# The hidden tiles of a two-layer decoder trunk, placed 128 bytes further along each partition

## Chip, core and metric

The kernel runs on one core of one Trainium2 chip. The metric is device time in microseconds (us), the median of several executions. The engines are named as in the profile: PE (TensorE matmuls), PEld (TensorE weight loads), DVE (VectorE), ACT (ScalarE), POOL (GpSimd), SP (SyncE).

## What is computed

A decoder trunk of two layers over 256 tokens of width 1024, all in float32. Each layer is an attention followed by an MLP, each with a residual and a layer norm:

```python
def squared_relu_mlp(x, w_up, w_down):
    return jnp.square(jax.nn.relu(x @ w_up)) @ w_down
...
        h = layer_norm(DEEPNORM_ALPHA * h + mix, ln1_g[layer], ln1_b[layer])
        h = layer_norm(DEEPNORM_ALPHA * h + squared_relu_mlp(h, w_up[layer], w_down[layer]),
                       ln2_g[layer], ln2_b[layer])
```

`w_up` is 1024 x 4096 and `w_down` 4096 x 1024 in each layer. Layer 0 has a differential attention, layer 1 a block-sparse one, which at 256 tokens is one causal block.

## The kernel before

**Products.** Every float32 operand of a large product is split into a rounded part and a remainder (`act_hi` and `act_lo`, `whi` and `wlo`, `h_hi` and `h_lo`), and `three` issues three matmuls into one PSUM bank: high by high, high by low, low by high. With `moving_w` the activation is the stationary operand (it is loaded into the array, 128 x 128) and the weights stream past it, 512 columns a matmul; L141, L142 and L143 are these three. Without it the weights are stationary and the activation streams, 256 columns a matmul: L145, L146 and L147.

**Weights.** The weights of both layers come as 96 units of 128 x 2048 through a ring of `raw` tiles; ACT rounds each half unit (`whi`, L103) and DVE subtracts (`wlo`, L115). `bg` issues that work between matmuls.

**The MLP.** `mlp` works through the 4096 hidden columns in eight chunks `c` of 512. The first two chunks are computed with tokens on the partitions (`up_rows`), squared (`square`: tiles `relu`, `sqr`) and transposed on PE (`up_turn`, L776). From chunk 2 on, `up(c, j)` computes half a chunk with the weights stationary, 48 matmuls of 256 columns, and `up_out` squares and splits it into `h_hi` and `h_lo`. `down(c, j)` multiplies the hidden chunk by `w_down`: hidden tiles stationary, weights moving, 24 matmuls of 512 columns a call, 48 for both `j` (half as many where it takes one half of the tokens). From chunk 3 on the order is written out by hand: `down(c - 3, 0)`, `down(c - 3, 1)`, `up(c, 0)`, `up(c, 1)`. In layer 1 the last quarter of the output is done in two pieces of 256 columns in the banks `ps_b` (`rest`).

**Places in SBUF.** The pools are stacked: constants (`act_hi`, `act_lo`, `xres`, `ident`), then the weights' pool (`raw`, `whi`, `wlo`, `bias`), then small tiles, then on top either the attention's pool or the MLP's, in the same bytes. Within a pool the tiles stand in the order in which their names are first asked for. In the MLP's pool that is `relu` (2 buffers of 2 KB a partition), `sqr` (2 of 2 KB), `h_hi` (3 of 4 KB), `h_lo` (3 of 4 KB). Counted in bytes from the start of a partition, every `whi`, `wlo` and `raw` tile begins 192 bytes past a multiple of 512; `act_hi`, `act_lo`, `xres`, `ident`, `relu`, `sqr`, `h_hi` and `h_lo` begin 128 bytes past one. In the attention's pool `t` begins 128 past a multiple and `o` 192 past. Each slice that a matmul takes starts a whole number of 512 bytes into its tile, so the slices stand as their tiles do.

Of the kernel before, what the change touches and what calls it, by code (L numbers as in the profile page):

```python
# [20 lines left out]
F32 = mybir.dt.float32  # L21
# [7 lines left out]
P = 128  # L29
# [23 lines left out]
def trunk(ctx: ExitStack, tc: tile.TileContext, x, first, units, lam_a, subln, rel_bias,  # L53
# [686 lines left out]
    def mlp(layer, u0, then):  # L740
# [3 lines left out]
        with tc.tile_pool(name=f"mlp{layer}", bufs=2) as pool:  # L744
            H, acc, rest, SQ = {}, {}, {}, {}

            def hidden(c):
                H[c] = (pool.tile([P, 4, S], F32R, name="h_hi", bufs=3),
                        pool.tile([P, 4, S], F32R, name="h_lo", bufs=3))
# [20 lines left out]
            def up_turn(c, h):  # L770
                if h == 0:
                    hidden(c)
                src = SQ.pop((c, h))
                pt = bank("c")
                for j in range(4):
                    nc.tensor.transpose(pt[:, j * P:(j + 1) * P], src[:, j * P:(j + 1) * P], ident)  # L776
                split_to(H[c][0][:, :, tokens(h)], H[c][1][:, :, tokens(h)],
                         pt.rearrange("p (j t) -> p j t", j=4))

            def up(c, j):  # L780
                if j == 0:
                    hidden(c)
                u = u0 + [0, 2, 4, 8, 12, 16, 20, 24][c] + j
                hi, lo = unit(u, k=NK)
                ps = bank("b")
                for m in range(2):
                    w = slice(m * P, (m + 1) * P)
                    for k in range(NK):
                        three(ps[:, m * S:(m + 1) * S], (hi[:, k, w], lo[:, k, w]),
                              (act[0][:, k], act[1][:, k]), False, 1 / 16, k == 0, k == NK - 1)  # L790
                used.add(u)
                SQ[c, j] = ps
# [110 lines left out]
    with tc.manual_schedule(engines=engines):  # L903
        attention(0, 0)
        mlp(0, 16, lambda: ln_params(1))
        attention(1, UNITS)
        mlp(1, UNITS + 16, None)
# [73 lines left out]
```

## Time and profile before

| | |
|---|---|
| median of 3 runs | 593.27 us (593.0 to 593.7) |
| the profiled execution, its own time | 593.63 us |
| its span, first to last instruction | 591.6 us |
| outside the span | 2.0 us |
| mean granted TensorE clock | 0.995 of full speed |
| PE busy | 580.2 us, 98% of the span |
| PEld busy | 515.6 us, 87% |
| DVE, ACT busy | 378.5 us, 318.3 us |
| DMA | 113.03 MB, 191 GB/s on average |

Matmuls overlap in the profile: the duration of one counts its way through the array, and the next starts before it ends. The pace of a stream of matmuls is therefore read from the starts of two of them and the number between, not from the durations.

### The profile page before, as it was taken

To read this page: it belongs to the slowest core of one execution; us is meant where nothing else is said; L and a number is where in the kernel's file an instruction comes from. 1 tells how busy PE (TensorE), PEld (TensorE's weight loads), DVE (VectorE), ACT (ScalarE), POOL (GpSimd) and SP (SyncE) were. 2 spreads that over 40 slices of the span, in tenths; PEclk is the share of its full clock that TensorE was granted. 3 is DMA by queue.
4 is the path that set the end of the run, shared out by engine and by line. 5 is a ranking of instruction groups with operands and counts; after the bars stand their busy time and mean duration, and the time that the engine had idled before them with its cause. 6 is when DMAs were issued, how large, how long until landed. Compare 5 with 4: busy or idle time off the path is not lost.

```text
span 591.6 us, 9649 instructions
## 1 busy us (share of the span) xinstructions
PE 580.2 (98%) x3768; PEld 515.6 (87%) x3768; DVE 378.5 (64%) x692; ACT 318.3 (54%) x540; POOL 13.1 (2%) x45
## 2 busy tenths in 40 slices
PE   9999999999999999999999999999999999999993
PEld 7999978889899899898889999878899899899883
DVE  5798778976744644543978677697785544554236
ACT  6676787257654655552447555642785564554100
POOL 2000020000000000000000000000000000000000
PEclk9999999999999999999999999999999999999998
DMA  8996736447745836755259744151798556553002
GB/s 300 327 337 229 243 116 212 174 150 268 271 172 207 277 126 237 248 168 191 83 170 344 256 150 155 54 178 36 242 324 288 175 183 214 187 170 107 1 0 71
DMA packets 35548, 113.03 MB, mean 191 GB/s; under 512 B 3872, under 2 KB 8880, under 8 KB 35504
## 3 DMA queue, kind: packets, MB, share of 16 engines
q1 hardware_dynamic: 34144, 107.95, 53.8%
q0 software_dynamic: 1152, 4.19, 2.4%
q8 instruction: 29, 0.48, 0.3%
q10 hardware_dynamic: 208, 0.29, 0.1%
q14 instruction: 15, 0.12, 0.1%
HBM read 111.35 MB, written 1.07 MB: 190 GB/s over the span
## 4 chain that ended last, share of the span: by engine, by line
PE 97%; DMA 1%; DVE 1%; ACT 0%; SPq 0%; issue 0%; DVEq 0%
PE ps_a L143 13%; PE ps_a L142 13%; PE ps_b L145 13%; PE ps_a L141 13%; PE ps_b L147 12%; PE ps_b L146 12%; PE ps_b L141 4%; PE ps_b L143 4%; PE ps_b L142 4%; PE ps_a L462 2%; PE ps_c L515 1%; PE ps_c L292 1%; DMA raw<-in_first 1%; PE ps_a L550 1%; PE ps_c L776 1%; PE ps_a L381 1%
## 5 line engine op out<-in xcount | busy, mean ns | idle before, releaser
L115 DVE TENSOR_TENSOR wlo<-raw,whi 128x1024 fp32r<-128x1024 f32 x188 | 222.8, 1220 | 55.1 <-ACT whi L103 54.7
L103 ACT ACTIVATE whi<-raw 128x1024 fp32r<-128x1024 f32 x188 | 190.1, 1052 | 71.6 <-PE ps_a L143 52.5
L145 PE MATMUL ps_b<-act_hi,whi 128*128 128x256 f32 x640 | 179.8, 281 | 0.0
L146 PE MATMUL ps_b<-act_lo,whi 128*128 128x256 f32 x640 | 177.5, 277 | 0.0
L147 PE MATMUL ps_b<-act_hi,wlo 128*128 128x256 f32 x640 | 177.5, 277 | 0.0
L145 PEld LDWEIGHTS ps_b<-act_hi,whi 128*128 128x128 f32 x640 | 120.2, 188 | 1.5 <-issue 0.7
L146 PEld LDWEIGHTS ps_b<-act_lo,whi 128*128 128x128 f32 x640 | 120.7, 189 | 0.5
L147 PEld LDWEIGHTS ps_b<-act_hi,wlo 128*128 128x128 f32 x640 | 120.3, 188 | 0.0
L143 PE MATMUL ps_a<-whi,h_lo 128*128 128x512 f32 x248 | 97.7, 394 | 0.0
L142 PE MATMUL ps_a<-wlo,h_hi 128*128 128x512 f32 x248 | 97.2, 392 | 0.0
L141 PE MATMUL ps_a<-whi,h_hi 128*128 128x512 f32 x248 | 96.5, 389 | 0.0
L74 DVE TENSOR_TENSOR h_lo<-sqr,h_hi 128x512 fp32r<-128x512 f32 x24 | 16.6, 693 | 77.7 <-ACT h_hi L72 77.7
L142 PEld LDWEIGHTS ps_a<-wlo,h_hi 128*128 128x128 f32 x248 | 46.6, 188 | 10.3
L141 PEld LDWEIGHTS ps_a<-whi,h_hi 128*128 128x128 f32 x248 | 46.6, 188 | 9.9
L143 PEld LDWEIGHTS ps_a<-whi,h_lo 128*128 128x128 f32 x248 | 46.6, 188 | 9.3
L753 ACT ACTIVATE relu<-ps_b 128x512 f32<-128x512 f32 x32 | 19.1, 596 | 65.9 <-PE ps_b L147 55.0
L482 ACT ACTIVATE t<-t,mx 128x256 f32<-128x256 f32 x64 | 28.4, 445 | 31.5 <-DVE mx L479 31.5
L141 PE MATMUL ps_b<-whi,act_hi 128*128 128x512 f32 x96 | 39.1, 407 | 0.0
L143 PE MATMUL ps_b<-whi,act_lo 128*128 128x512 f32 x96 | 37.7, 393 | 0.0
L142 PE MATMUL ps_b<-wlo,act_hi 128*128 128x512 f32 x96 | 37.6, 391 | 0.0
L141 PE MATMUL ps_a<-whi,act_hi 128*128 128x512 f32 x80 | 32.3, 403 | 0.0
L142 PE MATMUL ps_a<-wlo,act_hi 128*128 128x512 f32 x80 | 31.5, 393 | 0.0
(140 smaller groups left out, 587.3 us busy)
## 6 DMA issues: line engine op xcount, KB each, us to landing
raw<-in_units SPq DMA_DIRECT2D x188, 512.0 KB, 4.6
bias<-scr SPq DMA_DIRECT2D x16, 256.0 KB, 5.3
lnp<-in_ln_g POOLq DMA_DIRECT2D x4, 512.0 KB, 4.5
lnp<-in_ln_b POOLq DMA_DIRECT2D x4, 512.0 KB, 5.4
raw<-in_first SPq DMA_DIRECT2D x5, 384.0 KB, 6.6
xres<-in_x SPq DMA_DIRECT2D x1, 1024.0 KB, 5.9
out<-xres SPq DMA_DIRECT2D x2, 256.0 KB, 2.1
out<-xres SPq DMA_DIRECT2D x4, 128.0 KB, 1.9
```

Source lines behind the costliest of these rows:

```text
L74: nc.vector.tensor_tensor(lo, src, hi.bitcast(F32), op=ALU.subtract)
L103: nc.scalar.activation(split[v][0][:, c], raws[state["head"]], AF.Copy)
L115: nc.vector.tensor_tensor(split[v][1][:, c], raws.pop(state["piece"]), split[v][0][:, c].bitcast(F32), op=ALU.subtract)
L141: nc.tensor.matmul(ps, a[0], w[0], start=start, stop=False)
L142: nc.tensor.matmul(ps, a[0], w[1], start=False, stop=False)
L143: nc.tensor.matmul(ps, a[1], w[0], start=False, stop=stop)
L145: nc.tensor.matmul(ps, w[0], a[0], start=start, stop=False)
L146: nc.tensor.matmul(ps, w[0], a[1], start=False, stop=False)
L147: nc.tensor.matmul(ps, w[1], a[0], start=False, stop=stop)
L462: nc.tensor.matmul(sc[m][:, c:c + n], a[r, q], b[r, :n], start=i == 0, stop=i == 2)
L482: nc.scalar.activation(t[:, m, s], t[:, m, s], AF.Exp, bias=mx[:, m, j:j + 1], accum_out=sm[:, m, j:j + 1])
L753: nc.scalar.activation(r, ps, AF.Relu)
```

## The change

One tile of 32 float32 a partition (128 bytes) is asked for first in the MLP's pool of each layer. Nothing reads or writes it. `relu`, `sqr`, `h_hi` and `h_lo` then begin 128 bytes later, at 256 past a multiple of 512; every tile of the lower pools stays where it was.

```diff
@@ -744,6 +744,8 @@
         with tc.tile_pool(name=f"mlp{layer}", bufs=2) as pool:
             H, acc, rest, SQ = {}, {}, {}, {}
 
+            pool.tile([P, 32], F32, name="pad", bufs=1)
+
             def hidden(c):
                 H[c] = (pool.tile([P, 4, S], F32R, name="h_hi", bufs=3),
                         pool.tile([P, 4, S], F32R, name="h_lo", bufs=3))
```

## Rows read from the trace of the kernel before

**Rows 1.** The page: busy time of the engines, and the chain that ended last by line.

```profile
PE 580.2 (98%) x3768; PEld 515.6 (87%) x3768; DVE 378.5 (64%) x692; ACT 318.3 (54%) x540; POOL 13.1 (2%) x45
...
PE ps_a L143 13%; PE ps_a L142 13%; PE ps_b L145 13%; PE ps_a L141 13%; PE ps_b L147 12%; PE ps_b L146 12%; PE ps_b L141 4%; PE ps_b L143 4%; PE ps_b L142 4%; PE ps_a L462 2%; PE ps_c L515 1%; PE ps_c L292 1%; DMA raw<-in_first 1%; PE ps_a L550 1%; PE ps_c L776 1%; PE ps_a L381 1%
```

**Rows 2.** Waits of PE, first and last of four: us in total, times, longest.

```profile
PE ps_c L186 <- DVE lnp L179: 1.2, 1, 1.2
...
PE ps_a L381 <- ACT whi L72: 0.2, 1, 0.2
```

**Rows 3.** Groups by line and shape, whole run: busy us, mean ns | idle before.

```profile
L143 PE MATMUL ps_a<-whi,h_lo 128*128 128x512 f32 x248 | 97.7, 394 | 0.0
L142 PE MATMUL ps_a<-wlo,h_hi 128*128 128x512 f32 x248 | 97.2, 392 | 0.0
L141 PE MATMUL ps_a<-whi,h_hi 128*128 128x512 f32 x248 | 96.5, 389 | 0.0
...
L776 PEld LDWEIGHTS ps_c<-ident,sqr 128*128 128x128 f32 x32 | 3.9, 140 | 0.8
...
L74 DVE TENSOR_TENSOR wlo<-raw,whi 128x512 fp32r<-128x512 f32 x5 | 3.5, 693 | 0.1
...
L292 PEld LDWEIGHTS ps_c<-ident,o 128*128 128x128 f32 x16 | 1.8, 140 | 1.8 <-ACT aT L524 0.8 <-ACT V L349 0.7
```

**Rows 4.** Timeline of PE, one pair of `down` calls: start us, duration us.

```profile
172.38 0.39 PE L142 MATMUL ps_a<-wlo,h_hi 128*128 128x512 f32 x1
...
182.68 0.39 PE L142 MATMUL ps_a<-wlo,h_hi 128*128 128x512 f32 x1
```

**Rows 5.** Timeline of PE, one pair of `up` calls that follows a `down`.

```profile
161.25 0.28 PE L145 MATMUL ps_b<-act_hi,whi 128*128 128x256 f32 x1
...
161.84 0.28 PE L147 MATMUL ps_b<-act_hi,wlo 128*128 128x256 f32 x1
...
172.04 0.28 PE L147 MATMUL ps_b<-act_hi,wlo 128*128 128x256 f32 x1
```

**Rows 6.** Timeline of PE, the pair of `up` calls for chunk 2.

```profile
138.73 0.28 PE L147 MATMUL ps_b<-act_hi,wlo 128*128 128x256 f32 x1
...
149.69 0.28 PE L147 MATMUL ps_b<-act_hi,wlo 128*128 128x256 f32 x1
```

**Rows 7.** Timeline of PE, end of layer 0's attention.

```profile
98.94 0.60 PE L292 MATMUL ps_c<-ident,o 128*128 128x128 f32 x4
...
99.85 0.40 PE L143 MATMUL ps_b<-whi,act_lo 128*128 128x512 f32 x1
...
111.05 0.40 PE L143 MATMUL ps_a<-whi,act_lo 128*128 128x512 f32 x1
```

**Rows 8.** Timeline of PE, the two 256-column pieces at the end of layer 1.

```profile
576.99 0.28 PE L141 MATMUL ps_b<-whi,h_hi 128*128 128x256 f32 x1
...
582.09 0.28 PE L141 MATMUL ps_b<-whi,h_hi 128*128 128x256 f32 x1
```

**Rows 9.** By tile (`h_hi`, `h_lo`, `relu`, `sqr`): ns min/median/max, first and last start.

```profile
L753 ACT ACTIVATE relu<-ps_b x32: 577/598/599, 120.0 to 549.7; 128x512 f32<-128x512 f32 x32
L755 ACT ACTIVATE sqr<-relu x32: 630/632/634, 120.6 to 550.3; 128x512 f32<-128x512 f32 x32
L72 ACT ACTIVATE h_hi<-sqr x24: 631/632/635, 145.6 to 551.0; 128x512 fp32r<-128x512 f32 x24
L74 DVE TENSOR_TENSOR h_lo<-sqr,h_hi x24: 691/693/694, 146.3 to 551.7; 128x512 fp32r<-128x512 f32 x24
L143 PEld LDWEIGHTS ps_a<-whi,h_lo x248: 187/188/188, 150.5 to 576.5; 128*128 128x128 f32 x124
```

**Rows 10.** Windows: length, busy us (instructions) of PE, PEld, DVE, ACT, POOL; granted clock, DMA, GB/s.

```profile
100.00:150.00 50.00, 50.00 (x281) 43.07 (x280) 40.10 (x63) 28.40 (x37) 1.17 (x2) 1.00 0.62 210
150.00:200.00 50.00, 50.00 (x319) 44.98 (x318) 27.88 (x27) 30.67 (x38) 0.00 (x0) 1.00 0.61 215
```

**Rows 11.** Timeline of DVE around the first `down`.

```profile
140.04 0.69 DVE L74 TENSOR_TENSOR h_lo<-ps_c,h_hi 128x512 fp32r<-128x512 f32 x1 [2.99 <-ACT h_hi L72]
```

## The prediction, made before the changed kernel was run

> **What bounds the kernel now.** I read the page first, for the busy shares and the chain that ended last, then the waits of PE, then the timeline of PE stretch by stretch. PE is busy for 98% of the span, and the chain is a list of matmul lines [rows 1]: the kernel lasts as long as PE needs to issue its 3768 matmuls. PE itself waits four times, the longest wait 1.2 us, and every one of the four is at the start of the program or around layer 0's attention; none has a tile of the MLP in it [rows 2]. So a change that only moves tiles can act in two ways: it changes the spacing of the matmuls that read those tiles, or it makes a producer of them so late that PE begins to wait.
>
> The spacing is what the reader should look at. In a pair of `down` calls the L142 matmuls that start at 172.38 and 182.68 are 45 matmuls apart (15 groups of three): 10.30 / 45 = 228.9 ns for 512 columns [rows 4]. In a pair of `up` calls the two L147 at 161.84 and 172.04 are 90 apart: 10.20 / 90 = 113.3 ns for 256 columns [rows 5]. But the same two kinds of stream also run at a second, slower beat. The `up` calls of chunk 2 take 10.96 us for 93 matmuls, 117.8 ns each [rows 6], and 48 matmuls of layer 0's output projection take 11.20 us, 233.3 ns each [rows 7]. So a matmul is about 4.4 ns (512 columns) or 4.5 ns (256 columns) dearer on the slow beat. The granted clock is 1.00 around both beats [rows 10], so the clock is not what separates them. Neither is the place of the operands: `up` of chunk 2 [rows 6] and `up` of chunk 3 [rows 5] read the same `act` tiles and weights' tiles that stand alike. A stream falls into a beat when it starts and keeps it: the first six starts of the `up` at 161.25 span 0.59 us, 118 ns each, and the rest of that stretch runs at 113.3 [rows 5].
>
> **The change part by part.**
>
> *Instructions.* The new tile is neither written nor read. No instruction, DMA or queue entry is added or moved: 0 us.
>
> *Matmuls with hidden tiles as the stationary operand.* These are 3 x 248 = 744 of 512 columns [rows 3] and 48 of 256 columns. Before, stationary tile and moving weights stand at 128 and 192 past a multiple of 512 bytes: the weights are 64 bytes ahead. After, it is 256 and 192: they are 64 bytes behind. The trace holds both arrangements, though not for 512 columns. In `up` the moving `act` stands at 128 and the stationary weights at 192, so the moving side is 64 bytes behind, as it will be in `down` after the change: 113.3 ns [rows 5]. In the last 48 matmuls of layer 1 the hidden tile is stationary and the weights move, 64 bytes ahead: the L141 at 576.99 and 582.09 are 45 apart, 5.10 / 45 = 113.3 ns [rows 8]. The two are the same to the resolution of the rows, and they differ in the relative place by just the 128 bytes of this change. I take 0 from this. The bounds: as a loss, that all 744 fall to the slow beat, 744 x 4.4 = 3.3 us. As a gain, that a 512-column matmul comes down to twice the 256-column one, 226.6 ns: 744 x 2.3 = 1.7 us.
>
> A page would allow a larger effect. The row gives 228.9 ns for 512 columns [rows 4]. The Trainium skill, "TensorE: Matmul & The Clock Gate", section "Wait — 56ns, not 53.3ns?", gives N / 2.4 + about 2.5 ns from start to start of matmuls back to back, measured there as 215.7 ns at 512 columns. By the page 13.2 ns of each gap would be a surplus, and if it came from where the two operands stand and the shift removed it, the sum would be an estimated 744 x 13.2 = 9.8 us less, 583.5 us. The row does not say where that surplus comes from.
>
> *Weight loads.* They take 187 to 188 ns with hidden tiles [rows 9], and loads are hidden under the running matmul. The transposes of `sqr` load in 140 ns from 128 past a multiple, and those of `o` in the same 140 ns from 192 past [rows 3]: 0 us for the 32 of them.
>
> *ACT and DVE.* Per half chunk `relu` 598, `sqr` 632, `h_hi` 632 and `h_lo` 693 ns [rows 9]; the subtraction of a weight of the same shape, whose tiles stand 64 bytes elsewhere, takes the same 693 ns [rows 3]. I take 0. The cover is large in any case. For chunk 0 the last `h_lo` is written from 140.04 us, done at 140.7 [rows 11], and the first `down` loads its `h_lo` at 150.5 [rows 9]: over 9 us of cover against 0.7 us of work. For chunk 7 the last `h_lo` is done at 551.7 + 0.7 = 552.4, and its `up` ended at about 549.7, when `relu` began [rows 9]; 48 matmuls of `down(5)` and 24 of one token half of chunk 6 come first, 72 x 228.9 ns = 16.5 us, so it is first read at about 566, 13 us after it is done. A producer would have to become nine us later before PE waits; without any cover a half chunk would cost the 2.6 us of these four instructions in a row.
>
> *Old neighbours.* The MLP's tiles lie where attention's tiles lay. Shifted by 128 bytes, the third `h_hi` reaches into the old `o`, the first `h_lo` into the old `V`. The transposes of `o` before the MLP are at 98.94 [rows 7], and `h_hi` from chunk 2 is first written at 145.6 [rows 9]: over 40 us lie between. 0 us.
>
> The sum is 0, against the 593.63 us of the profiled execution (span 591.6 and 2.0 outside). That execution lies 0.36 us above the median of 593.27. I predict the median, 593.3.
>
> **The rivals.**
>
> *Slower: the hidden tiles push the matmuls to the slow beat.* The place is the boundary where `down` starts after `up`, the price 4.4 ns a matmul, and it decides as soon as one more stall per matmul appears between the load and the moving stream. For it: both beats occur in this trace with 512 columns [rows 4, 7], and 512 columns with the new relative place are not in the trace. Against it: rows 5 and 8 as above. If the `down` calls alone are hit: 593.3 + 3.3 = 596.6. A `down` on the slow beat may also hand it to the five `up` pairs that follow one in each layer, 10 x about 90 matmuls x 4.5 = 4.1 us more: 600.7.
>
> *Faster: the shift ends part of the 228.9.* For it: 512 columns cost 2.3 ns more than twice 256. Against: that surplus may belong to the length of the stream, and nothing in the trace ties it to the tiles' place. With 1.7 us gained: 591.6. The page named above would allow 583.5; I give that 0.02 of the gain's chance, since the rows show no 512-column stream faster than 228.9 ns.
>
> *The beats after a transpose flip.* Chunk 2's `up` follows the transposes of `sqr`, and it is slow in both layers (I show layer 0's). The moved `sqr` could start it on the fast beat: 2 x 93 x 4.5 = 0.8 us, 592.4, which stays within the bound of no change.
>
> *The change does nothing at all,* if the tile were placed behind the others: 593.3, the same forecast by another way.
>
> **How the numbers follow.** What a measurement here can tell from no change is about 0.2%, 1.2 us. The forecast of no effect, with the flip after the transposes and the tile that moves nothing, has 0.68: 592.1 to 594.5. The slow beat has 0.19, of which `down` alone 0.12 and `down` with `up` 0.07. A gain over 1.2 us has 0.13. So faster 0.13, same 0.68, slower 0.19. The range goes from 592.0 to 596.8: it takes in the forecast and the slow beat in the `down` calls, 0.80, and leaves out the gain and the slow beat everywhere.
>
> **What would show it.** Right: in the profile after, a pair of `down` calls still has 228.9 ns between starts, the mean of the L141 to L143 groups stays at 389 to 394 ns, `up` after a `down` stays at 113.3, and PE waits no more than before. Wrong on the slow side: `down` at about 233, the means of these groups near 398. Wrong on the fast side: `down` below 228. The prediction is wrong above all if a 512-column stream reacts to a place that a 256-column stream does not notice.

## The result, and the profile after

The changed kernel takes 598.59 us (median of 5 runs, 597.66 to 599.16) against 593.70 us (median of 5, 593.00 to 593.86): 1.0082 times the time before, interval 1.0071 to 1.0094. It is slower by 0.8%. The forecast of no effect, 593.3 us, was wrong, and the time lies above the range, which ended at 596.8. The rival "the hidden tiles push the matmuls to the slow beat" is what happened, as far as the times go; its two prices, 596.6 and 600.7, lie on either side of the measured time.

The profiled execution has its own time of 599.16 us and a span of 597.1, 5.5 us longer than before. The page shows the same picture: PE is busy for 98% of the span and the chain is PE's matmul lines.

```profile
PE 584.9 (98%) x3768; PEld 517.0 (87%) x3768; DVE 378.1 (63%) x692; ACT 318.9 (53%) x540; POOL 12.9 (2%) x45
...
PE ps_a L141 13%; PE ps_a L143 13%; PE ps_a L142 13%; PE ps_b L145 13%; PE ps_b L147 12%; PE ps_b L146 12%; PE ps_b L141 4%; PE ps_b L143 4%; PE ps_b L142 4%; PE ps_a L462 2%; PE ps_c L515 1%; PE ps_c L292 1%; DMA raw<-in_first 1%; PE ps_a L550 1%; PE ps_c L778 1%; PE ps_a L381 1%
```

The waits of PE are the same four (us in total, times, longest). None belongs to the MLP. The one that grew, by 0.8 us against [rows 2], is the first weight tile at the start of the program, ahead of anything that the change touches; the first 256-column stream starts 0.5 us later for it (at 17.07 us, before at 16.56).

```profile
PE ps_c L186 <- DVE lnp L179: 1.2, 1, 1.2
PE ps_a L381 <- ACT whi L72: 1.0, 1, 1.0
PE ps_c L292 <- ACT aT L524: 0.6, 1, 0.6
PE ps_c L292 <- ACT V L349: 0.4, 1, 0.4
```

Beyond that half microsecond PE does not wait longer: the matmuls themselves are further apart. By line and shape, the three groups of `down` (means 389, 392 and 394 ns in [rows 3]) are now:

```profile
L141 PE MATMUL ps_a<-whi,h_hi 128*128 128x512 f32 x248 | 98.2, 396 | 0.0
L143 PE MATMUL ps_a<-whi,h_lo 128*128 128x512 f32 x248 | 98.1, 395 | 0.0
L142 PE MATMUL ps_a<-wlo,h_hi 128*128 128x512 f32 x248 | 98.0, 395 | 0.0
```

The timeline of PE gives the spacing. Below stand, in this order, the `up` pair of chunk 3 (two L145 that are 87 matmuls apart), a `down` pair (two L141, 39 apart), the `up` pair of chunk 4 (87 apart), layer 1's first attention projection (87 apart) and the 256-column pieces at the end (39 apart).

```profile
162.66 0.28 PE L145 MATMUL ps_b<-act_hi,whi 128*128 128x256 f32 x1
...
172.52 0.28 PE L145 MATMUL ps_b<-act_hi,whi 128*128 128x256 f32 x1
...
174.25 0.40 PE L141 MATMUL ps_a<-whi,h_hi 128*128 128x512 f32 x1
...
183.36 0.39 PE L141 MATMUL ps_a<-whi,h_hi 128*128 128x512 f32 x1
184.76 0.28 PE L145 MATMUL ps_b<-act_hi,whi 128*128 128x256 f32 x1
...
195.01 0.28 PE L145 MATMUL ps_b<-act_hi,whi 128*128 128x256 f32 x1
...
320.29 0.28 PE L145 MATMUL ps_b<-act_hi,whi 128*128 128x256 f32 x1
...
330.15 0.28 PE L145 MATMUL ps_b<-act_hi,whi 128*128 128x256 f32 x1
...
582.96 0.28 PE L141 MATMUL ps_b<-whi,h_hi 128*128 128x256 f32 x1
...
587.55 0.28 PE L141 MATMUL ps_b<-whi,h_hi 128*128 128x256 f32 x1
```

`down`: 9.11 / 39 = 233.6 ns, where [rows 4] has 228.9; over all stretches it is 233.2 to 233.4, and no `down` of either layer is at 229. It is slow straight after an `up` on the fast beat (chunk 3: 9.86 / 87 = 113.3). Of the ten `up` pairs that follow a `down`, six are still at 113.3 and four have gone to the slow beat, those of chunks 4 and 6 in each layer (10.25 / 87 = 117.8). The last 48 matmuls go from 113.3 [rows 8] to 4.59 / 39 = 117.7. Two stretches that read no hidden tile slow down as well: the 39 matmuls of `act` right after layer 0's last `down` go from 228.6 to 233.4, and layer 1's second projection (48 matmuls) from 113.2 to 117.6. One stretch went the other way: layer 1's first projection runs at 9.86 / 87 = 113.3, and ran at 10.25 / 87 = 117.8 before:

```profile
317.16 0.28 PE L145 MATMUL ps_b<-act_hi,whi 128*128 128x256 f32 x1
...
327.41 0.28 PE L145 MATMUL ps_b<-act_hi,whi 128*128 128x256 f32 x1
```

The sum, each stretch counted from its first start to the first start of what follows it: `down` 3.2 us, the four `up` pairs 4 x 0.41 = 1.6, the last 48 matmuls 0.2, the 39 of `act` 0.2, layer 1's two projections 0.2 - 0.4, the start of the program 0.5: 5.5 us, against 5.5 of span. Without the start it is 5.0, and the medians differ by 4.9. The granted clock is 0.996 over the span, as before (0.995).

### The profile page after: what moved, and what is told of

Read it like the earlier page. It is cut to its first block, busy times and chain, and to the rows that moved or that the text cites. A ratio compares the mean times of both kernels' runs of the same rounds, so it can differ in the third digit from the quotient of the medians.

```text
span 597.1 us, 9649 instructions
## 1 busy us (share of the span) xinstructions
PE 584.9 (98%) x3768; PEld 517.0 (87%) x3768; DVE 378.1 (63%) x692; ACT 318.9 (53%) x540; POOL 12.9 (2%) x45
## 4 chain that ended last, share of the span: by engine, by line
PE 97%; DMA 1%; DVE 1%; ACT 0%; SPq 0%; issue 0%; DVEq 0%
PE ps_a L141 13%; PE ps_a L143 13%; PE ps_a L142 13%; PE ps_b L145 13%; PE ps_b L147 12%; PE ps_b L146 12%; PE ps_b L141 4%; PE ps_b L143 4%; PE ps_b L142 4%; PE ps_a L462 2%; PE ps_c L515 1%; PE ps_c L292 1%; DMA raw<-in_first 1%; PE ps_a L550 1%; PE ps_c L778 1%; PE ps_a L381 1%
## 5 line engine op out<-in xcount | busy, mean ns | idle before, releaser
L145 PE MATMUL ps_b<-act_hi,whi 128*128 128x256 f32 x640 | 180.2, 282 | 0.0
L145 PEld LDWEIGHTS ps_b<-act_hi,whi 128*128 128x128 f32 x640 | 120.4, 188 | 1.5 <-issue 0.7
L141 PE MATMUL ps_a<-whi,h_hi 128*128 128x512 f32 x248 | 98.2, 396 | 0.0
L141 PEld LDWEIGHTS ps_a<-whi,h_hi 128*128 128x128 f32 x248 | 46.6, 188 | 10.7
L141 PE MATMUL ps_b<-whi,act_hi 128*128 128x512 f32 x96 | 39.2, 408 | 0.0
L141 PE MATMUL ps_a<-whi,act_hi 128*128 128x512 f32 x80 | 32.4, 405 | 0.0
L143 PE MATMUL ps_a<-whi,act_lo 128*128 128x512 f32 x80 | 31.5, 394 | 0.0
```

Source lines behind the costliest of these rows:

```text
L141: nc.tensor.matmul(ps, a[0], w[0], start=start, stop=False)
L143: nc.tensor.matmul(ps, a[1], w[0], start=False, stop=stop)
L145: nc.tensor.matmul(ps, w[0], a[0], start=start, stop=False)
```

## Experiments

**Which of the moved tiles it is, and seen from where.** Four kernels, each an edit of the kernel before.

A pad of 512 bytes instead of 128: the tiles move four times as far and stand at 128 past a multiple of 512 again.

```diff
+            pool.tile([P, 128], F32, name="pad", bufs=1)
```

> The pad in the MLP's pool is 512 bytes instead of 128, so its tiles move four times as far but stand at 128 past a multiple of 512 again. Place theory (where a hidden tile begins within 512 bytes, seen from the weights, sets the spacing of the 512-column matmuls): back to before, 593.7 us, down at 228.9 ns a matmul. Rival, any shift upsets the beats (another order of overlaps with attention's old tiles, another way into the stream): about 598 us or some third value, down not at 228.9 throughout.

Measured: 593.91 us, ratio 1.0006 (0.9997 to 1.0015). Two L141 of a `down` pair, 39 apart, are 8.93 us apart, 229.0 ns:

```profile
173.78 0.39 PE L141 MATMUL ps_a<-whi,h_hi 128*128 128x512 f32 x1
...
182.71 0.39 PE L141 MATMUL ps_a<-whi,h_hi 128*128 128x512 f32 x1
```

A move as such is harmless; new overlaps with attention's old tiles are not the cause.

Only `h_hi` and `h_lo` moved by 128 bytes, then only `relu` and `sqr`:

```diff
 # hidden tiles only
             def hidden(c):
+                if c == 0:
+                    pool.tile([P, 32], F32, name="padh", bufs=1)
 # relu and sqr only: 128 bytes ahead of them, 384 more ahead of h_hi
+            pool.tile([P, 32], F32, name="pad", bufs=1)
...
             def hidden(c):
+                if c == 0:
+                    pool.tile([P, 96], F32, name="padh", bufs=1)
```

> Only h_hi and h_lo stand 128 bytes further; relu and sqr keep their places. Place theory: the whole loss stays, 598 to 599 us, down at 233.3 ns. Rival, the transposes of the moved sqr start the streams on the slow beat, which is then handed on: 593.7 us, down at 228.9.

> relu and sqr stand 128 bytes further, h_hi and h_lo 512 bytes further, which is the same place within 512. Place theory: 593.7 us within 1 us, down at 228.9; up of chunk 2 may change its beat by up to 0.8 us for both layers. Rival of the transposes of sqr: 598 to 599 us.

Measured: hidden tiles only, 598.63 us, 1.0088 (1.0074 to 1.0102), `down` at 9.10 / 39 = 233.3 ns, the same four `up` pairs slow. `relu` and `sqr` only: 593.49 us, 1.0000 (0.9991 to 1.0009), `down` at 8.92 / 39 = 228.7. The transposes of `sqr` and ACT's work on `relu` and `sqr` have no part in it. The rows are of the first of the two:

```profile
173.96 0.40 PE L141 MATMUL ps_a<-whi,h_hi 128*128 128x512 f32 x1
...
183.06 0.39 PE L141 MATMUL ps_a<-whi,h_hi 128*128 128x512 f32 x1
```

Everything from `act_hi` upwards moved by 128 bytes, the weights too:

```diff
+    const.tile([P, 32], F32, name="padc")
     act = (const.tile([P, NK, S], F32R, name="act_hi"), const.tile([P, NK, S], F32R, name="act_lo"))
```

> Everything from act_hi upwards, weights included, stands 128 bytes further, so the hidden tiles are at 256 past a multiple of 512 as in the change and the weights at 320: the relative places are those of before. Relative place decides: 593.7 us, down at 228.9. Rival, the hidden tile's own place (256 past a multiple) decides: down at 233.3, 597 us or more.

Measured: 593.72 us, 1.0006 (0.9997 to 1.0015). The hidden tiles stand at 256 past a multiple of 512, as in the change, and `down` is at 8.93 / 39 = 229.0:

```profile
194.57 0.39 PE L141 MATMUL ps_a<-whi,h_hi 128*128 128x512 f32 x1
...
203.50 0.39 PE L141 MATMUL ps_a<-whi,h_hi 128*128 128x512 f32 x1
```

So it is not the hidden tiles' own place but their place seen from tiles that were moved with them here. Of these `act` drops out by the kernels further down: there the weights and the hidden tiles move together, away from `act`, and `down` stays at 228.9. What is left is the weights' pool, which holds `whi` and `wlo`, that PE reads, and `raw` and `bias`, that it does not.

Could writes of the other engines or of DMA do it, by meeting PE's reads? The profile of the changed kernel has 10 us of `down` in which DVE, ACT and POOL are idle and the DMA share is 0.01. The spacing there is 9.10 / 39 = 233.3 all the same, so the writes are not needed for it, and the tiles that count are `whi` and `wlo`:

```profile
560.00:570.00 10.00, 10.00 (x45) 8.05 (x44) 0.00 (x0) 0.00 (x0) 0.00 (x0) 1.00 0.01 2
...
560.55 0.39 PE L141 MATMUL ps_a<-whi,h_hi 128*128 128x512 f32 x1
...
569.65 0.40 PE L141 MATMUL ps_a<-whi,h_hi 128*128 128x512 f32 x1
```

**The other places.** Pads of 64, 256, 384 and 192 bytes (`[P, 16]`, `[P, 64]`, `[P, 96]`, `[P, 48]` in the same line).

> Pad of 64 bytes: the hidden tiles begin at 192 past a multiple of 512, exactly where the weights begin. If the loss comes from hidden tiles standing behind the weights, this is the border case: down at 228.9 ns and 593.5 us if the border belongs to the good side, 233.3 and 598 us if to the bad. If two reads that start at the same place collide most, it is the worst of all: over 233.3 ns, over 599 us.

> Pad of 256 bytes: hidden tiles at 384, weights at 192, so 192 bytes behind. If the pattern repeats every 256 bytes this is the place of before (64 ahead): 593.5 us, down at 228.9. If it repeats only every 512 and being behind is what costs: 598 us, down at 233.3.

> Pad of 384 bytes: hidden tiles at 0, weights at 192, so 192 bytes ahead. If the pattern repeats every 256 bytes this is the place of the change (64 behind): 598 us, down at 233.3. If it repeats every 512 and being ahead is good: 593.5 us, down at 228.9.

> Pad of 192 bytes: the stationary hidden tiles begin 128 bytes behind the weights, the one place of the four within 256 bytes not yet seen (64 ahead gave 228.9 ns in down, level 226.7, 64 behind 233.3). If the spacing rises steadily from level to behind: at or over 233.3 ns, 598 us or more. If the two sides of half the period are alike: between 228.9 and 233.3, 594 to 598 us. The last 48 matmuls of 256 columns go with it (113.3 ns at 64 ahead, 117.8 at 64 behind, 119.8 level).

Measured, with the change and the kernel before in their places; "ahead" and "behind" say where the weights' tiles begin, seen from the hidden tiles, within 256 bytes. "Level" means that both begin at the same byte within 256. The spacings are means of a steady stretch in ns, good to about 0.3; the ratio's interval stands in brackets.

| pad, bytes | weights | `down` | ten `up` pairs after a `down` | last 48 | us | ratio |
|---|---|---|---|---|---|---|
| 0 (before) | 64 ahead | 228.9 | 113.3 all | 113.3 | | 1 |
| 64 | level | 226.7 | 117.8 all | 120.0 | 595.23 | 1.0028 (1.0018 to 1.0038) |
| 128 (the change) | 64 behind | 233.3 | 117.8 in four | 117.8 | 598.59 | 1.0082 (1.0071 to 1.0094) |
| 192 | 128 away | 232.1 to 232.5 | 117.8 all | 118.7 | 600.07 | 1.0103 (1.0088 to 1.0118) |
| 256 | 64 ahead again | 228.9 | 113.3 all | 113.3 | 593.56 | 1.0000 (0.9991 to 1.0009) |
| 384 | 64 behind again | 233.3 | 117.8 in four | 117.8 | 598.90 | 1.0090 (1.0075 to 1.0105) |

The two places that were tried twice, 256 bytes apart, agree, down to which `up` pairs are slow; for the other two the period of 256 bytes is taken over, not shown. The level place is the best for `down`, and the whole gain of it and more is lost in the `up` pairs behind it. Timeline of the pad of 64 bytes: a `down` pair (39 apart, 8.84 / 39 = 226.7), the `up` pair after it (87 apart, 10.24 / 87 = 117.7), the last 48 (39 apart, 4.68 / 39 = 120.0):

```profile
173.42 0.39 PE L141 MATMUL ps_a<-whi,h_hi 128*128 128x512 f32 x1
...
182.26 0.39 PE L141 MATMUL ps_a<-whi,h_hi 128*128 128x512 f32 x1
183.65 0.28 PE L145 MATMUL ps_b<-act_hi,whi 128*128 128x256 f32 x1
...
193.89 0.28 PE L145 MATMUL ps_b<-act_hi,whi 128*128 128x256 f32 x1
...
579.08 0.28 PE L141 MATMUL ps_b<-whi,h_hi 128*128 128x256 f32 x1
...
583.76 0.28 PE L141 MATMUL ps_b<-whi,h_hi 128*128 128x256 f32 x1
```

The same pair of `down` rows with the pad of 256 bytes (8.93 / 39 = 229.0):

```profile
173.59 0.39 PE L141 MATMUL ps_a<-whi,h_hi 128*128 128x512 f32 x1
...
182.52 0.39 PE L141 MATMUL ps_a<-whi,h_hi 128*128 128x512 f32 x1
```

and with the pad of 192 bytes (9.07 / 39 = 232.6):

```profile
174.49 0.40 PE L141 MATMUL ps_a<-whi,h_hi 128*128 128x512 f32 x1
...
183.56 0.39 PE L141 MATMUL ps_a<-whi,h_hi 128*128 128x512 f32 x1
```

**Does each load pay for itself?** Only `h_lo` moved, by 128 bytes; then `h_hi` and `h_lo` set apart, one of them level with the weights.

```diff
 # only h_lo by 128 bytes; with [P, 16] h_lo is level and h_hi as before
+                hi = pool.tile([P, 4, S], F32R, name="h_hi", bufs=3)
+                if c == 0:
+                    pool.tile([P, 32], F32, name="padl", bufs=1)
+                H[c] = (hi, pool.tile([P, 4, S], F32R, name="h_lo", bufs=3))
 # h_hi level: [P, 16] as the pool's first tile and [P, 48] ahead of h_lo
```

> Only h_lo stands 128 bytes further. One load in three of down then has the place of the change. If each load pays for its own place, a third of the loss of down: 248 x 4.4 ns = 1.1 us, 594.6 us, down near 230.4 on average. If the beat belongs to the stream as a whole, all or nothing: 593.5 or 597 to 599 us.

> h_hi 64 bytes ahead of the weights as before, h_lo level with them. If each load pays for its own place: down (2 x 228.9 + 226.7) / 3 = 228.2 ns, 0.5 us less, 593.2 us, with up as before at 113.3. If the stream follows one of the two as a whole: 228.9 or 226.7, and up at 117.8 behind a down of 226.7, 593.7 or 595.2 us.

> h_hi level with the weights, h_lo 64 bytes ahead. Each load for itself: (2 x 226.7 + 228.9) / 3 = 227.4 ns, 1.1 us less, 592.6 us if up stays at 113.3, 596 us if it goes to 117.8. As a whole: 228.9 or 226.7.

Measured. Only `h_lo` by 128: 596.35 us, 1.0047 (1.0030 to 1.0064); `down` at 9.09 / 39 = 233.1, all ten `up` pairs at 9.86 / 87 = 113.3. One misplaced load in three costs `down` as much as three, and the difference to the change lies for the most part in the `up` pairs (1.7 us).

```profile
183.76 0.28 PE L145 MATMUL ps_b<-act_hi,whi 128*128 128x256 f32 x1
...
193.62 0.28 PE L145 MATMUL ps_b<-act_hi,whi 128*128 128x256 f32 x1
...
195.37 0.40 PE L141 MATMUL ps_a<-whi,h_hi 128*128 128x512 f32 x1
...
204.46 0.40 PE L141 MATMUL ps_a<-whi,h_hi 128*128 128x512 f32 x1
```

`h_lo` level: 597.78 us, 1.0074 (1.0062 to 1.0087), `down` at 8.95 / 39 = 229.5 (two L141 at 173.17 and 182.12), all ten `up` pairs at 117.8. `h_hi` level: 594.41 us, 1.0012 (1.0003 to 1.0021), `down` at 9.00 / 39 = 230.8 (two L141 at 194.98 and 203.98), all ten at 113.3. Both expectations are missed: neither do the loads add up one by one, nor does the stream take one tile's value.

**Does the rule hold for other operands?** The weights and all above them moved away from `act_hi` and `act_lo`, by 64 and by 128 bytes; the hidden tiles keep their place relative to the weights. Seen from `act`, the weights then begin 128 away, and 64 behind within 256.

```diff
     nlam = const.tile([P, 1], F32, name="nlam")
+    const.tile([P, 16], F32, name="padw")   # 64 bytes; [P, 32]: 128 bytes
```

> 64 bytes between the constants and the weights: weights, hidden tiles and attention's tiles move together, only act, xres and ident stay. Down keeps its relative place: 228.9 ns. The act tiles stand 128 bytes from the weights instead of 64. If the rule of relative place holds for any operand: the output and value products of attention (512 columns, act stationary) take the spacing that a pad of 192 bytes shows for down, and up (256 columns, act moving) a new one for all its matmuls. Rival, only the hidden tiles react: 593.6 us, up and attention as before.

> 128 bytes between the constants and the weights: hidden tiles stay 64 ahead of the weights, act tiles stand 192 ahead, which is 64 behind within 256. Rule of relative place: down 228.9 ns; attention's 576 matmuls of 512 columns with act stationary at 233.3 (2.3 us more); up with its weights 64 ahead of the moving act now always at 113.3 ns, no slow stretch (1.7 us less). Together 594 us. Rival, only hidden tiles react: 593.6 us with the slow up stretches where they were.

Measured. By 64: 604.94 us, 1.0183 (1.0168 to 1.0198). Nine of the ten `up` pairs are at 10.44 / 87 = 120.0 (two L145 at 187.22 and 197.66), the tenth at 118.7. The long streams with `act` stationary are at 232.3 to 233.4; 232.5 was expected.

By 128: 600.60 us, 1.0113 (1.0098 to 1.0128). The long streams with `act` stationary, the weights now 64 behind, are at 233.1 to 233.4, all six of them; before, five of the six were at 228.6 to 229.1 and only the one of [rows 7] at 233.3. The rows show one of the five, in layer 1: two L141 42 apart, 9.61 / 42 = 228.8 before and 9.80 / 42 = 233.3 here.

```profile
306.15 0.39 PE L141 MATMUL ps_a<-whi,act_hi 128*128 128x512 f32 x1
...
315.76 0.39 PE L141 MATMUL ps_a<-whi,act_hi 128*128 128x512 f32 x1
```

`down`, at its old relative place, is at 8.93 / 39 = 229.0. That half came as expected, and 233.3 at 64 behind now holds for another stationary tile. The other half did not: of the streams with `act` moving, whose weights now stand 64 on the other side of `act`, the ten `up` pairs after a `down` are at 10.25 / 87 = 117.8, and only chunk 2's, in both layers, are at 113.4. The last 48, at their old relative place, are at 4.60 / 39 = 117.9.

```profile
310.13 0.40 PE L141 MATMUL ps_a<-whi,act_hi 128*128 128x512 f32 x1
...
319.93 0.39 PE L141 MATMUL ps_a<-whi,act_hi 128*128 128x512 f32 x1
...
175.66 0.39 PE L141 MATMUL ps_a<-whi,h_hi 128*128 128x512 f32 x1
...
184.59 0.39 PE L141 MATMUL ps_a<-whi,h_hi 128*128 128x512 f32 x1
185.99 0.28 PE L145 MATMUL ps_b<-act_hi,whi 128*128 128x256 f32 x1
...
196.24 0.28 PE L145 MATMUL ps_b<-act_hi,whi 128*128 128x256 f32 x1
...
585.16 0.28 PE L141 MATMUL ps_b<-whi,h_hi 128*128 128x256 f32 x1
...
589.76 0.28 PE L141 MATMUL ps_b<-whi,h_hi 128*128 128x256 f32 x1
```

The attempt to put the good halves together, this kernel with the hidden tiles level:

> As the one before, and the hidden tiles level with the weights: down 226.7 ns (1.7 us less), up always at 113.3, attention at 233.3: 592.3 us, 0.2% below before. If up after a level down starts on the slow beat here too: 595 us or more.

Measured: 599.72 us, 1.0100 (1.0083 to 1.0117). `down` is at 8.84 / 39 = 226.7 and attention at 233.3 as expected, but `up` is at 10.24 / 87 = 117.7 and the last 48 at 120.0. That is the "if" of the expectation, but the level `down` is not shown to be its cause: `up` was at 117.8 in the kernel above too, behind a `down` of 229.0. No version tried beats the kernel before beyond its interval.

**The way into a stream.** All places as before; ahead of each `up` pair from chunk 3 on, four transposes that nothing reads.

```diff
+                pt = bank("c")
+                for j in range(4):
+                    nc.tensor.transpose(pt[:, j * P:(j + 1) * P], ident, ident)
                 for j in range(2):
                     up(c, j)
```

> Places as before; four transposes of ident into a bank that nothing reads stand ahead of each of the ten up pairs that follow a down (40 matmuls more, about 0.44 us for each four with the restart, 4.4 us in all). If the way into a stream picks the beat: the ten up pairs run at 117.8 ns as chunk 2's do behind its transposes, 10 x 93 x 4.5 = 4.2 us more, 602 us. If down's place hands its beat on: up stays at 113.3, 598 us.

Measured: 604.96 us, 1.0195 (1.0180 to 1.0211). All ten `up` pairs run at 10.25 / 87 = 117.8 although no tile moved, and the `down` pairs after such an `up` at 9.10 / 39 = 233.3. Only each layer's first `down`, which follows the transposes of `sqr`, stays at 228.9. The 3 us above the expectation are that: 648 matmuls x 4.4 = 2.9 us. Not all of the 1.0195 is the beat: the transposes themselves take 0.36 us a set, 3.6 us for the ten.

```profile
162.21 0.28 PE L145 MATMUL ps_b<-act_hi,whi 128*128 128x256 f32 x1
...
172.46 0.28 PE L145 MATMUL ps_b<-act_hi,whi 128*128 128x256 f32 x1
...
174.22 0.40 PE L141 MATMUL ps_a<-whi,h_hi 128*128 128x512 f32 x1
...
183.32 0.40 PE L141 MATMUL ps_a<-whi,h_hi 128*128 128x512 f32 x1
```

So at 64 ahead a 512-column stream has both beats, and what PE did just before can pick one. At 64 behind, in the change and in the pad of 384 bytes, every `down` was at 233.2 to 233.4, after a fast `up`, after a slow one and after transposes alike.

## Why the prediction was wrong

**The step that failed** is "Matmuls with hidden tiles as the stationary operand", at "I take 0 from this". It carried the evidence of 256-column streams over to 512-column ones. A 256-column stream has two beats at 64 bytes on either side: 64 ahead, the last 48 matmuls run at 113.3 before and at 117.9 with the weights moved by 128 bytes; `up` has both beats at its old place (113.3 and 117.8 in [rows 5, 6]) and both at the other (113.4 in chunk 2 and 117.8 in the ten pairs, with the weights moved by 128). The two equal values of [rows 5, 8] were therefore two streams that happened to be on the same beat, and could not say what the place does to `down`. The 512-column streams react to the place itself: straight after the same fast `up`, `down` runs at 228.9 ns with the weights 64 ahead and at 233.3 with them 64 behind, and over the four places of 64 bytes it runs at 226.7, 228.9, 233.3 and about 232.3. The term was put at 0; it measured 3.2 us in `down`, and the streams around it added 1.8.

**"Neither is the place of the operands"**, in the first part, was half right. Both beats do occur at one place (the transposes ahead of `up` show it with nothing moved), but from that it does not follow that the place is indifferent: it decides which beats a stream can take. At 64 behind only the slow one was seen in 512-column streams. That a stream "keeps" the beat into which it falls is not so from the first matmul on: in [rows 5] itself the first starts are 118 ns apart and the rest 113.3.

**The bounds** were right in size. Against the loss bound of 3.3 us for `down` stand 3.2 measured. The gain bound, 226.6 ns for 512 columns, is reached by the level place, 226.7. The `up` pairs as a further loss were priced at 4.1 us for all ten; four of ten fell, 1.6 us. So the total lies between the rival's two prices, which is in part luck: nothing in the rival says that four would fall. "A `down` on the slow beat may hand it on" does not explain which fell: with only `h_lo` moved `down` is slow and all `up` pairs fast, with level tiles `down` is at its best and all of them slow.

**The range** took in the slow beat in `down` alone and left out its `up` pairs. With 0.19 for the slower side, and with 512 columns at the new place named as what the trace does not hold, it should have reached to 600.7.

**Right:** no instruction was added and none moved; the transposes and the work of ACT and DVE cost nothing (`relu` and `sqr` alone moved: 1.0000); the old neighbours cost nothing (the pad of 512 bytes); PE has no new wait in the MLP. The rival of the beats after a transpose did not occur in the change, where chunk 2's `up` stays at 117.8; with the pads of 64 and 192 bytes it did, in both layers (113.4, and 11.40 us down to 10.98 in layer 0 with 64).

**The two pages.** The row of before lies 13.2 ns above the 215.7 ns that the Trainium skill, "TensorE: Matmul & The Clock Gate", section "Wait — 56ns, not 53.3ns?", has for 512 columns. For the most part this is not a matter of the place: the best of the four places gives 226.7, still 11.0 ns above the page's figure. And the Trainium skill, "SBUF — State Buffer", section "Who interferes with whom", gives PE two independent read ports, one for the moving operand and one for weight loads, and says that PE never waits on anyone. Read so, the relative place of the two should not matter; here it moves the spacing from 226.7 to 233.3 ns, and the measurement decides.

**What stays open.** Why the place matters at all, why in steps within 256 bytes, and how the way into a stream picks its beat, is not shown: the trace has no finer view of a load against the stream under it. The stall between the load and the moving stream, of which the rival spoke, would fit the spacings, but no row shows it. Nor is it shown why the slow `up` pairs of the change are just those of chunks 4 and 6.

## What to carry to other kernels

Where PE is the bound and every matmul loads a new stationary tile, the places of the two operands within 256 bytes of a partition are a parameter of the kernel, worth up to 1.8% among the kernels tried here in which only places differ, and an allocation anywhere below can change it. Move a pad of 64, 128 and 192 bytes through each pool and read the spacing of the starts, stretch by stretch: a gain in one stretch (226.7 in `down`) can be lost in the next (117.8 in `up`). And do not take the spacing of one shape as evidence for another, least of all when the same trace shows that the shape has two beats.

## What the hardware showed that was not expected

The spacing of fp32r matmuls with 512 moving columns depends on where the stationary tile begins relative to the moving one. In `down`, with the weights seen from the hidden tiles, it is 228.9 ns (64 ahead), 226.7 (level), 233.3 (64 behind) and 232.1 to 232.5 (128 away); the two places tried again 256 bytes further, 64 ahead and 64 behind, gave the same. At 64 ahead a stream can also run at 233.3: `down` does behind a slow `up`, and [rows 7] have another case. The spacing does not depend on the common place: both moved by 128 bytes, 229.0. One load in three at the bad place costs as much as three (233.1).

With 256 columns level is bad (120.0 ns), so is 128 away (118.7 to 120.0), and 64 bytes on either side allows 113.3 and 117.8 ns, steady over whole stretches. What PE did just before can decide between them: four transposes ahead of a stream turn it from the one to the other.
